# Low parts of streamed weights by adding transfers onto -hi, and attention scores of head pairs on two row halves of the array

## Chip, cores and metric

The kernel runs on one core of a Trainium2 chip. The metric is the device time of one execution in microseconds, the median of several runs. The engines are TensorE (PE; its weight loads are shown apart as PEld), VectorE (DVE), ScalarE (ACT), GpSimd (POOL) and SyncE (SP), which issues most transfers. PSUM is the memory that TensorE writes; SBUF holds everything else on the core.

## What is computed

Two layers of a hybrid block, for two request groups that share the weights: a prompt of 512 tokens and a sample group of 32 tokens with a past of 256. All of it is float32. Cut to what the change touches:

```python
h = rms_norm(x, g_mix)
glu_a, glu_b, rq, rk, rv, rg, fq, fk, fv, ff, gates = split_in(h @ w_in)
# A: GLU, causal depthwise conv (31 taps), LayerNorm, swish, w_conv_out
# B: retention, 8 heads, chunkwise, GroupNorm, gate, w_ret_out
# C: forgetting attention, 8 heads of 64:
fq = rms_norm(fq.reshape(b, t, H_FOX, DH_FOX), g_q_fox)
fk = rms_norm(fk.reshape(b, t, H_FOX, DH_FOX), g_k_fox)
s = jnp.einsum('bthd,bshd->bhts', q, k) * (DH_FOX ** -0.5)
s = jnp.where(mask, s + cum_q - cum_k, -jnp.inf)
p = jax.nn.softmax(s, axis=-1)
o = jnp.einsum('bhts,bshd->bthd', p, v)
# merged = sum of gated branches; x = x + merged @ w_out
# FFN: a, gb = split(rms_norm(x) @ w_ffn_up); x = x + (gelu(dwconv3(a)) * gb) @ w_ffn_down
```

## The kernel before

Activations lie transposed, channels on the 128 partitions and the T = 544 tokens (32 of the sample group, then 512 of the prompt) along the free dimension, so each matrix product is a row of gemms that give 128 output channels for all tokens.

**The gemms.** A float32 operand is used as two float32r values, hi (the value as ScalarE writes it to float32r) and lo = value - hi. `gemm` (L287) makes three passes for each of 8 blocks of 128x128 weights and each half of the tokens (272 columns): weight hi x activation hi, weight hi x activation lo, weight lo x activation hi. That is 48 matmuls (L305) into one PSUM tile `acc`, of which there are two.

**The weight stream.** `Stream` (L182) brings the weights in 146 units per layer, 1024 columns (512 KB) each, in the order of use. `load_part` (L190) loads a unit from the DRAM tensor `wpack` into `raw` (two buffers), issued by SyncE. `split_part` (L197) then fills `hi` and `lo` (three buffers each): ScalarE copies raw to hi (L203), and GpSimd subtracts hi from raw (L204). For the first two units VectorE subtracts. A `slot` (L311) takes unit u, asks for the split of unit u + 2 and the load of unit u + 4 (`ahead`, L225), and runs the gemm; so a unit's hi and lo are written while the gemm before the last runs, as soon as the gemm that used their buffers is over.

**The attention branch (C).** `qk_done` (L586) takes one of 4 + 4 gemm results (two heads of q or k each, on 64 partitions apiece), normalizes them, and splits the prompt part into hi and lo. For a matmul with 128 rows it stacks operands: SyncE copies hi and lo by four transfers per result into `qst[e]` (own half: q hi, other half: q lo) and `kst[e]` (k hi in both halves); the low part of k goes to `klo`. `p_scores` (L743) handles one head and one block of 128 queries: one matmul of 128 rows gives q hi x k hi + q lo x k hi (L751), a second one of 64 rows adds q hi x k lo (L752). The columns are the keys up to the block's end, at least 256. Then VectorE adds the bias and the mask (L755, L756), `softmax` runs on VectorE and ScalarE (L685), `p_trans` transposes (L763, copied out by ScalarE at L765) and `p_pv` multiplies by v (L781).

**What sets the order.** `fox_side` (L663) is a generator; its steps, and the conv of branch A (`conv_side`, L473, whose taps are L483 on VectorE), are called from hooks inside the gemms, two or three per gemm. In step k it runs the scores of item k, the transposes of item k - 3 and the product with v of item k - 4. The tile framework then places the instructions of each engine. ScalarE, VectorE and GpSimd each work through their own list in that order; SyncE does the same with its transfers. The retention side (L868 its scores, on row halves of the array; L892, L898, L904 its products) follows after the attention side.

Of the kernel before, what the change touches and what calls it, by code (L numbers as in the profile page):

```python
# [11 lines left out]
F32 = mybir.dt.float32  # L12
F32R = mybir.dt.float32r
AF = mybir.ActivationFunctionType
ALU = mybir.AluOpType
AX = mybir.AxisListType

P = 128
DEPTH = 2
D = 1024  # L20
NS = 32
NP = 512
T = NS + NP
# [88 lines left out]
def trunk(ctx, tc, x_in, wpack, wff, consts, params, s_conv, s_ret, s_cache, s_clf, s_ffn,  # L112
          y_out, o_conv, o_ret, o_fk, o_fv, o_lf, o_ffn):
    nc = tc.nc
    PS = bass.MemoryType.PSUM
    mm = nc.tensor.matmul
    act = nc.scalar.activation
    vtt = nc.vector.tensor_tensor
    stt = nc.vector.scalar_tensor_tensor
    gtt = nc.gpsimd.tensor_tensor  # L120
    dma = nc.sync.dma_start
# [12 lines left out]
    def Q(dt=F32):  # L134
        return qpool.tile([P, 4, T], dt, tag="q", name="q")

    def Wt(n=T):
        t = wpool.tile([P, CU], F32, tag="w", name="w")
        return t[:, :n]

    def Wr(n=T):
        t = wpool.tile([P, CU], F32R, tag="w", name="wr")
        return t[:, :n]
# [7 lines left out]
    def psS_t():  # L151
        return psS.tile([P, 512], F32, tag="s", name="s")
# [29 lines left out]
    class Stream:  # L182
# [14 lines left out]
        def split_part(self, u, i, sub, n=2):  # L197
            if i == 0:
                self.hl[u] = [upool.tile([P, UW], F32R, tag=t, name=t, bufs=3) for t in ("hi", "lo")]
                self.ns += 1  # L200
            hi, lo = self.hl[u]
            sl = slice(i * UW // n, (i + 1) * UW // n)
            act(hi[:, sl], self.raw[u][:, sl], AF.Copy)  # L203
            sub(lo[:, sl], self.raw[u][:, sl], hi[:, sl].bitcast(F32), op=ALU.subtract)  # L204
            if i == n - 1:
                self.raw.pop(u)

# [4 lines left out]
        def split(self, upto):  # L212
            while self.ns <= min(upto, DEPTH * NU - 1):
                self.load(self.ns)
                self.split_part(self.ns, 0, gtt, 1)

        def take(self):
            u = self.at
# [51 lines left out]
    def after(fn, lag=1):  # L270
        later.append([lag, fn])
# [39 lines left out]
    def slot(rhs, done, lo_last=False):  # L311
        blocks = ws.take()
        ws.ahead()
        tick()
        done(gemm(blocks, rhs, lo_last))
# [10 lines left out]
    def head_mean(src):  # L326

        hi, lo = Wr(), Wr()
        act(hi, src, AF.Copy)  # L329
        vtt(lo, src, hi.bitcast(F32), op=ALU.subtract)  # L330

        def product():
            res = []
            for h in range(2):
                p = psS_t()[:, :HN]
                mm(p, blkr, half(hi, h), start=True, stop=False)
                mm(p, blkr, half(lo, h), start=False, stop=True)
                res.append(p)
            return res

        return product

    def rsqrt(out, parts, m=1):

        y2 = Wt(out.shape[-1])
        n = parts[0].shape[-1]
        for i, v in enumerate(parts):
            act(out[:, i * n : (i + 1) * n], v, AF.Abs_reciprocal_sqrt, scale=1.0 / m, bias=epst)
        act(y2, out, AF.Square, scale=math.sqrt(0.5 / m))  # L349
        for i, v in enumerate(parts):  # L350
            y = y2[:, i * n : (i + 1) * n]
            stt(y, v, EPS * m, y, op0=ALU.add, op1=ALU.mult)  # L352
        stt(out, y2, 1.5, out, op0=ALU.subtract, op1=ALU.mult, reverse0=True)  # L353
# [71 lines left out]
    for l in range(DEPTH):  # L425
# [159 lines left out]

        def qk_done(j, gcol, out):  # L586
            def done(acc):
                qr = Wr()
                q = qr.bitcast(F32)
                R_norm.evict(q, acc)  # L590
                sq = Wt()
                act(sq, q, AF.Square)
                mean = head_mean(sq)

                def fin():
                    y = Wt()
                    rsqrt(y, mean())
                    stt(q, q, gcol, y, op0=ALU.mult, op1=ALU.mult)
                    is_k = out is not None
                    nc.gpsimd.tensor_copy(qks[:, is_k, j, :], q[:, 0:NS])  # L600
                    if is_k:
                        dma(out[:, j, :], q)
                        hi = Wr(NP)
                        act(hi, q[:, NS:T], AF.Copy)
                        gtt(klo[:, j, NS:T], q[:, NS:T], hi.bitcast(F32), op=ALU.subtract)
                    else:
                        hi, lo = Wr(NP), qr[:, NS:T]
                        act(hi, q[:, NS:T], AF.Copy)
                        gtt(lo, q[:, NS:T], hi.bitcast(F32), op=ALU.subtract)
                    for e in range(2):  # L610
                        own = slice(e * 64, e * 64 + 64)
                        far = slice(64 - e * 64, 128 - e * 64)
                        dst = (kst if is_k else qst)[e]
                        dma(dst[own, j, NS:T].bitcast(F32), hi[own].bitcast(F32))
                        dma(dst[far, j, NS:T].bitcast(F32), (hi if is_k else lo)[own].bitcast(F32))

                after(lambda: after(fin, 1), 1)

            return done
# [24 lines left out]
        gq8 = spool.tile([P, 1], F32, tag="gq8", name="gq8")  # L644
        nc.vector.tensor_scalar(gq8, pcol(P_GQ), 0.125, None, op0=ALU.mult)
        qks = Wt(8 * NS).rearrange("p (a j n) -> p a j n", a=2, j=4)
        qst = [Q(F32R) for _ in range(2)]
        for j in range(4):
            slot(rhs, qk_done(j, gq8, None))
        kst = [Q(F32R) for _ in range(2)]  # L650
        klo = Q(F32R)
        for j in range(4):
            slot(rhs, qk_done(j, pcol(P_GK), o_fk[l]))
        fv = vtile()
# [3 lines left out]
            slot(rhs, v_done(fv, fvs, j, o_fv[l]))  # L658


        foh, fol = qst

        def fox_side():  # L663
            cqs = spool.tile([P, 2], F32, tag="cqs", name="cqs", bufs=1)
            cks = [Wt(PAST + NS) for _ in range(2)]
            for g in range(2):
                for i in range(4):
                    h = g * 4 + i
# [73 lines left out]

            def p_scores(it):  # L743
                h, qb = it["h"], it["qb"]
                r = (h % 2) * 64
                n = (qb + 1) * P
                c = ck(h)
                p = psS_t()
                qs = qst[h % 2][:, h // 2, NS + qb * P : NS + n]
                nn = max(n, 256)  # L750
                mm(p[:, :nn], qs, kst[h % 2][:, h // 2, NS : NS + nn], start=True, stop=False)  # L751
                mm(p[:, :nn], qs[r : r + 64], klo[r : r + 64, h // 2, NS : NS + nn], start=False, stop=True)  # L752
                L = Wt(512)
                it["L"] = L
                stt(L[:, :n], c[:, :n], CM[:, h, qb : qb + 1], p[:, :n], op0=ALU.subtract, op1=ALU.subtract)  # L755
                vtt(L[:, n - P : n], L[:, n - P : n], cmask, op=ALU.add)  # L756
                softmax(L, n)
# [29 lines left out]
            for pr in range(4):  # L787
                for qb in range(4):
                    a = dict(f=(p_scores, p_trans, p_pv), h=2 * pr, qb=qb)
                    b = dict(f=(p_scores, p_trans, p_pv), h=2 * pr + 1, qb=qb)  # L790
                    a["mate"] = b
                    items += [a, b]
            n = len(items)
            for k in range(n + 4):
                for lag, f in ((4, 2), (3, 1), (0, 0)):
                    if 0 <= k - lag < n:
                        it = items[k - lag]
                        it["f"][f](it)
                yield
# [264 lines left out]
            side.append(ret_side())  # L1064
            side.append(gn_side())

        branch(2, qst)

        def need():
            drain(side)  # L1070
# [226 lines left out]
```

## Time and profile before

| | us |
|---|---|
| runs before (3) | 2033.06, 2039.91, 2041.58; median 2039.91 |
| profiled execution | 2039.84 |
| its span, first to last instruction | 2038.1 |
| busy: PE / DVE / POOL / ACT | 1969.1 / 1225.7 / 900.7 / 788.2 |
| mean granted TensorE clock | 0.991 |

The profile is one execution recorded by hardware. Busy is the time in which an engine has an instruction in work; matmuls overlap, and what they cost is read from start to start. The stretches of one layer are roughly, in the first: the input and the projections up to 125 us, the attention and retention sides beside their gemms from 125 to 420, the gates and the output projection to 575, and the FFN to 1025, where the second layer's first gemms follow. In a group's line stand the count, the busy time, the mean duration of one in ns, and the idle time of the engine ahead of them with what ended it; in a timeline the start, the duration, and in brackets the idle time ahead.

### The profile page before, as it was taken

The page shows a single profiled execution, that of the slowest core. Times are in us where ns is not written, and L with a number is a line of the kernel's source. Part 1 is how long each engine was busy: PE and PEld are TensorE (multiplying, and loading weights), DVE is VectorE, ACT ScalarE, POOL GpSimd, SP SyncE. Part 2 cuts the span into 40 slices and gives each one's busy share as a digit, 9 for nine tenths or more (in the row PEclk, how much of TensorE's full clock was granted, in tenths as well). Part 3 has the DMA queues.
Part 4 walks back from the last instruction along what each step waited for, and adds up shares of the span by engine and source line. Part 5 has one row for each costly group of instructions (what it writes and reads, how often), then busy time and mean ns, then how long its engine had stood idle before and what let it go on. Part 6 is the DMA issues. An engine that isn't in the chain of part 4 may idle for free.

```text
span 2038.1 us, 37239 instructions
## 1 busy us (share of the span) xinstructions
PE 1969.1 (97%) x15768; PEld 1913.6 (94%) x15768; DVE 1225.7 (60%) x1641; ACT 788.2 (39%) x1172; POOL 900.7 (44%) x580
## 2 busy tenths in 40 slices
PE   8999998999999999999999888989999999999999
PEld 7987888999999999999999877889999999999999
DVE  5587989666355660466326979995653656505640
ACT  4354552264334331233335445523452343313331
POOL 4463544244444444444444645432444344444442
PEclk9999999999999999999999999999999999999999
DMA  5353312122232222222433622112223322222232
GB/s 200 92 174 108 94 48 76 58 73 87 90 127 90 87 89 89 86 91 87 131 112 105 182 85 88 53 56 67 81 83 101 120 83 85 93 83 94 83 105 76
DMA packets 69075, 194.22 MB, mean 95 GB/s; under 512 B 14012, under 2 KB 15660, under 8 KB 68524
## 3 DMA queue, kind: packets, MB, share of 16 engines
q1 hardware_dynamic: 68908, 191.84, 29.2%
q8 instruction: 124, 2.03, 0.4%
q14 instruction: 43, 0.35, 0.1%
HBM read 169.07 MB, written 9.89 MB: 88 GB/s over the span
## 4 chain that ended last, share of the span: by engine, by line
PE 71%; DVE 22%; ACT 3%; issue 3%; DMA 1%; POOL 0%; SPq 0%; DVEq 0%; ACTq 0%; POOLq 0%
PE acc L305 68%; DVE w L483 10%; DVE w L756 1%; DVE q L324 1%; ACT hi L203 1%; DVE w L755 1%; DVE w L394 1%; DVE mn L687 1%; DVE w L353 1%; PE s L752 0%; DVE w L352 0%; DVE q L843 0%; ACT q L323 0%; DVE w L873 0%; DVE q L1019 0%
## 5 line engine op out<-in xcount | busy, mean ns | idle before, releaser
L305 PE MATMUL acc<-q,hi 128*128 128x272 f32 x9344 | 1789.6, 291 | 23.3 <-ACT q L323 9.0
L305 PEld LDWEIGHTS acc<-q,hi 128*128 128x128 f32 x9344 | 1475.3, 189 | 42.8 <-issue 9.4
L305 PE MATMUL acc<-q,lo 128*128 128x272 f32 x4672 | 1349.6, 289 | 0.0
L204 POOL TENSOR_TENSOR lo<-raw,hi 128x1024 fp32r<-128x1024 f32 x290 | 714.4, 2464 | 849.4 <-ACT hi L203 811.6
L305 PEld LDWEIGHTS acc<-q,lo 128*128 128x128 f32 x4672 | 883.0, 189 | 0.0
L203 ACT ACTIVATE hi<-raw 128x1024 fp32r<-128x1024 f32 (+1 forms) x293 | 309.4, 1056 | 735.4 <-PE acc L305 601.7
L483 DVE SCALAR_TENSOR_TENSOR w<-w,par 128x574 f32<-128x574 f32 x208 | 247.4, 1190 | 3.5
L1179 DVE TENSOR_TENSOR q<-acc,q 128x544 f32<-128x544 f32 x32 | 23.2, 725 | 208.9 <-PE acc L305 208.9
L1146 DVE SCALAR_TENSOR_TENSOR w<-w,par 128x546 f32<-128x546 f32 x44 | 93.6, 2128 | 42.9 <-ACT w L1145 42.9
L394 DVE TENSOR_TENSOR w<-acc,R 128x544 f32<-128x544 f32 x78 | 56.1, 720 | 95.5 <-PE acc L305 95.4
L321 DVE TENSOR_TENSOR q<-w,q 128x544 fp32r<-128x544 f32 x44 | 92.4, 2099 | 31.9 <-ACT q L320 31.9
L1148 ACT ACTIVATE w<-w 128x546 f32<-128x546 f32 x44 | 29.1, 662 | 129.7 <-DVE w L1147 129.6
L689 ACT ACTIVATE w<-w,mn 128x128 f32<-128x128 f32 (+4 forms) x68 | 38.0, 559 | 81.4 <-DVE mn L687 79.1
L324 DVE SCALAR_TENSOR_TENSOR q<-q,par 128x544 fp32r<-128x544 f32 x24 | 49.0, 2042 | 22.4 <-ACT q L323 22.4
L1141 POOL COPY fb<-w 128x2 f32<-128x2 f32 x44 | 8.1, 185 | 117.8 <-DVE w L1138 117.8
L1138 DVE TENSOR_TENSOR w<-acc,R 128x32 f32<-128x32 f32 x44 | 8.4, 192 | 83.2 <-PE acc L305 83.0
L813 POOL TENSOR_TENSOR w<-w,cst 128x544 f32<-128x544 f32 x16 | 26.2, 1641 | 65.7 <-DMA w<-q 59.7
L692 ACT ACTIVATE w<-w,rs 128x128 f32<-128x128 f32 (+4 forms) x68 | 37.9, 557 | 32.1 <-DVE rs L691 31.7
L490 POOL TENSOR_TENSOR w<-w 128x574 f32<-128x574 f32 x24 | 43.4, 1809 | 12.8 <-ACT w L486 11.2
L330 DVE TENSOR_TENSOR wr<-w,wr 128x544 fp32r<-128x544 f32 x24 | 27.2, 1133 | 33.3 <-ACT wr L329 33.3
L352 DVE SCALAR_TENSOR_TENSOR w<-s,w 128x272 f32<-128x272 f32 (+1 forms) x60 | 23.7, 436 | 38.1 <-ACT w L349 38.1
L1018 DVE SCALAR_TENSOR_TENSOR w<-w,acc 128x544 f32<-128x544 f32 x32 | 23.0, 720 | 37.3 <-PE acc L305 37.0
(207 smaller groups left out, 1563.2 us busy)
## 6 DMA issues: line engine op xcount, KB each, us to landing
raw<-in_wpack_dram SPq DMA_DIRECT2D x291, 512.0 KB, 3.3
q<-wr SPq DMA_DIRECT2D x64, 128.0 KB, 2.4
w<-in_x_dram SPq DMA_DIRECT2D x16, 272.0 KB, 4.2
w<-q SPq DMA_DIRECT2D x64, 68.0 KB, 3.0
ck<-cscr SPq DMA_DIRECT2D x16, 256.0 KB, 3.4
out_dram<-wr SPq DMA_DIRECT2D x8, 272.0 KB, 2.4
out_dram<-w SPq DMA_DIRECT2D x8, 272.0 KB, 2.6
xn<-q SPq DMA_DIRECT2D x8, 272.0 KB, 4.0
```

The costliest lines, as they stand in the source:

```text
L203: act(hi[:, sl], self.raw[u][:, sl], AF.Copy)
L204: sub(lo[:, sl], self.raw[u][:, sl], hi[:, sl].bitcast(F32), op=ALU.subtract)
L305: mm(acc[:, h, :HN], w, half(x, h), start=(i == 0 and j == 0), stop=(i == n - 1 and j == len(passes) - 1))
L321: vtt(lo, src, hi.bitcast(F32), op=ALU.subtract)
L324: stt(lo, src, scale, hi.bitcast(F32), op0=ALU.mult, op1=ALU.subtract)
L394: vtt(two(out), acc, two(self.R), op=ALU.mult)
L483: stt(c, u[:, k : k + CO], pcol(w + k), c, op0=ALU.mult, op1=ALU.add)
L490: gtt(p, p, t, op=ALU.add)
L689: act(L[:, :n], L[:, :n], AF.Exp, scale=-1.0, bias=mn, accum_out=sm)
L692: act(L[:, :n], L[:, :n], AF.Copy, scale=rs)
L1146: stt(c, a[:, 1 : 1 + FO], pcol(w + 1), c, op0=ALU.mult, op1=ALU.add)
L1148: act(c, c, AF.Gelu)
```

## The change

First, for all units but the first two, ScalarE writes hi and then lo = -hi (a second pass over 1024 columns, scale -1), and GpSimd issues a transfer that adds the unit's weights from DRAM onto lo. GpSimd's subtraction is gone; `raw` is read by ScalarE alone. Second, the stacked operands and the transfers that fill them are gone: q and k keep hi and lo in `qhl` and `khl`, and the even head's call of `p_scores` makes the scores of both heads of a pair by six matmuls of 64 rows, in turn on the upper and the lower half of the array, into two PSUM tiles. The product with v runs five steps behind instead of four, so the side has one step more.

```diff
@@ split_part, split
             act(hi[:, sl], self.raw[u][:, sl], AF.Copy)
-            sub(lo[:, sl], self.raw[u][:, sl], hi[:, sl].bitcast(F32), op=ALU.subtract)
+            if sub is None:
+
+                act(lo[:, sl], hi[:, sl].bitcast(F32), AF.Copy, scale=-1.0)
+                nc.gpsimd.dma_start(lo[:, sl], wpack[u][:, sl], accum_op=ALU.add)
+            else:
+                sub(lo[:, sl], self.raw[u][:, sl], hi[:, sl].bitcast(F32), op=ALU.subtract)
...
-                self.split_part(self.ns, 0, gtt, 1)
+                self.split_part(self.ns, 0, None, 1)
@@ qk_done
-                qr = Wr()
-                q = qr.bitcast(F32)
+                q = Wt()
...
-                        hi = Wr(NP)
-                        act(hi, q[:, NS:T], AF.Copy)
-                        gtt(klo[:, j, NS:T], q[:, NS:T], hi.bitcast(F32), op=ALU.subtract)
-                    else:
-                        hi, lo = Wr(NP), qr[:, NS:T]
-                        act(hi, q[:, NS:T], AF.Copy)
-                        gtt(lo, q[:, NS:T], hi.bitcast(F32), op=ALU.subtract)
-                    for e in range(2):
-                        own = slice(e * 64, e * 64 + 64)
-                        far = slice(64 - e * 64, 128 - e * 64)
-                        dst = (kst if is_k else qst)[e]
-                        dma(dst[own, j, NS:T].bitcast(F32), hi[own].bitcast(F32))
-                        dma(dst[far, j, NS:T].bitcast(F32), (hi if is_k else lo)[own].bitcast(F32))
+                    hi, lo = (khl if is_k else qhl)
+                    act(hi[:, j, NS:T], q[:, NS:T], AF.Copy)
+                    gtt(lo[:, j, NS:T], q[:, NS:T], hi[:, j, NS:T].bitcast(F32), op=ALU.subtract)
...
-        qst = [Q(F32R) for _ in range(2)]
+        qhl = [Q(F32R) for _ in range(2)]
...
-        kst = [Q(F32R) for _ in range(2)]
-        klo = Q(F32R)
+        khl = [Q(F32R) for _ in range(2)]
@@ p_scores
-                p = psS_t()
-                qs = qst[h % 2][:, h // 2, NS + qb * P : NS + n]
-                nn = max(n, 256)
-                mm(p[:, :nn], qs, kst[h % 2][:, h // 2, NS : NS + nn], start=True, stop=False)
-                mm(p[:, :nn], qs[r : r + 64], klo[r : r + 64, h // 2, NS : NS + nn], start=False, stop=True)
+                if h % 2 == 0:
+
+                    nn = max(n, 256)
+                    ps = [psS_t(), psS_t()]
+                    for i, (a, b) in enumerate(((0, 0), (0, 1), (1, 0))):
+                        for e in range(2):
+                            own = slice(e * 64, e * 64 + 64)
+                            mm(ps[e][:, :nn], qhl[a][own, h // 2, NS + qb * P : NS + n],
+                               khl[b][own, h // 2, NS : NS + nn], start=(i == 0), stop=(i == 2))
+                    it["p"], it["mate"]["p"] = ps
+                p = it["p"]
@@ fox_side, the steps
-            for k in range(n + 4):
-                for lag, f in ((4, 2), (3, 1), (0, 0)):
+            for k in range(n + 5):
+                for lag, f in ((3, 1), (5, 2), (0, 0)):
```

The order on three engines shows where it moves instructions. Line numbers of after differ by a few from those of before (L203 is the same; L206 and L207 are the two new lines; L310 is the gemm's matmul, L747 the scores', L761 the transposes', L779 the product with v, L1143 and L1146 the two ScalarE steps of the FFN that were L1145 and L1148, L325 the hi copy that was L320, L1139 and L1140 the small GpSimd copies that were L1141 and L1142).

ScalarE in the FFN of the first layer, before (hi, raw and lo are the weight stream's tiles, w and q working tiles):

```order
L203 ACTIVATE hi<-raw 128x1024
L1145 ACTIVATE w<-w,par 128x546
L1148 ACTIVATE w<-w 128x546
L203 ACTIVATE hi<-raw 128x1024
L320 ACTIVATE q<-w 128x544
```

and after:

```order
L203 ACTIVATE hi<-raw 128x1024
L206 ACTIVATE lo<-hi 128x1024
L1143 ACTIVATE w<-w,par 128x546
L1146 ACTIVATE w<-w 128x546
L203 ACTIVATE hi<-raw 128x1024
L325 ACTIVATE q<-w 128x544
L206 ACTIVATE lo<-hi 128x1024
```

Of each two units one has its lo right behind its hi, ahead of the FFN's steps; the other has it behind L325.

GpSimd at the same place, before:

```order
L204 TENSOR_TENSOR lo<-raw,hi 128x1024
L1141 COPY fb<-w 128x2
L204 TENSOR_TENSOR lo<-raw,hi 128x1024
L1142 COPY fb<-w 128x2
L1136 COPY w<-sf 128x2
L1137 MEMSET w 128x2
```

and after:

```order
L207 DMA lo<-in_wpack_dram 128x1024
L1139 COPY fb<-w 128x2
L1140 COPY fb<-w 128x2
L207 DMA lo<-in_wpack_dram 128x1024
L1134 COPY w<-sf 128x2
L1135 MEMSET w 128x2
```

Each transfer stands about where a subtraction stood; one of the small copies moved from behind the second to ahead of it.

TensorE in the attention side, before, at a block of 384 keys and the next (s is a PSUM tile of scores, t of transposes, o of the product with v; the gemm's matmuls between are left out by taking rows that follow each other):

```order
L781 MATMUL o<-w,q 64x128 x2
L763 MATMUL t<-cst,w 128x128 x2
L751 MATMUL s<-q 128x384
L752 MATMUL s<-q 128x384
L305 MATMUL acc<-q,hi 128x272 x2
L305 MATMUL acc<-q,lo 128x272
```

and after, at the next block, of 512 keys:

```order
L761 MATMUL t<-cst,w 128x128 x2
L779 MATMUL o<-w,q 64x128 x2
L747 MATMUL s<-q 128x512 x6
L310 MATMUL acc<-q,hi 128x272 x2
L310 MATMUL acc<-q,lo 128x272
```

The two matmuls per head became six per pair of heads, with nothing between them here; the next head's turn brings none, and the transposes moved ahead of the product with v. Of the 32 groups of six in the program, six are cut: into three and three with other rows between (four of them), or into three, two and one (two).

More of the change, by code (lines that the diff above doesn't have):

```diff
@@ L658, in trunk @@
             slot(rhs, v_done(fv, fvs, j, o_fv[l]))
-        foh, fol = qst
+        foh, fol = qhl
         def fox_side():
@@ L744, in p_scores @@
                 h, qb = it["h"], it["qb"]
-                r = (h % 2) * 64
                 n = (qb + 1) * P
                 c = ck(h)
-                p = psS_t()
-                qs = qst[h % 2][:, h // 2, NS + qb * P : NS + n]
-                nn = max(n, 256)
-                mm(p[:, :nn], qs, kst[h % 2][:, h // 2, NS : NS + nn], start=True, stop=False)
-                mm(p[:, :nn], qs[r : r + 64], klo[r : r + 64, h // 2, NS : NS + nn], start=False, stop=True)
+                if h % 2 == 0:
[8 more added lines that the diff above has]
+                p = it["p"]
                 L = Wt(512)
@@ L1065, in start_ret @@
             side.append(gn_side())
-        branch(2, qst)
+        branch(2, qhl)
         def need():
```

## Prediction

> **What bounds the kernel now.** I read the page's first part and its chain, then the busy table by stretch, then what TensorE waits for.
>
> ```profile
> span 2038.1 us, 37239 instructions
> ...
> PE 1969.1 (97%) x15768; PEld 1913.6 (94%) x15768; DVE 1225.7 (60%) x1641; ACT 788.2 (39%) x1172; POOL 900.7 (44%) x580
> ...
> PE acc L305 68%; DVE w L483 10%; DVE w L756 1%; DVE q L324 1%; ACT hi L203 1%; DVE w L755 1%; DVE w L394 1%; DVE mn L687 1%; DVE w L353 1%; PE s L752 0%; DVE w L352 0%; DVE q L843 0%; ACT q L323 0%; DVE w L873 0%; DVE q L1019 0%
> ```
>
> TensorE is the bound: it is idle for 2038.1 - 1969.1 = 69 us of the span. The change leaves the matmuls of the big gemms (L305) as they are. In the chain the only other entry of weight is VectorE's conv step L483.
>
> ```profile
> core 0: us, PE busy (x) PEld busy (x) DVE busy (x) ACT busy (x) POOL busy (x), PEclk, DMA share, GB/s
> 125.00:420.00 295.00, 273.32 (x2256) 249.54 (x2255) 247.29 (x354) 128.62 (x251) 128.42 (x65) 0.97 0.27 84
> 630.00:1025.00 395.00, 395.00 (x3151) 394.84 (x3151) 189.60 (x232) 129.39 (x153) 178.38 (x153) 1.00 0.29 96
> 1135.00:1430.00 295.00, 270.18 (x2250) 245.45 (x2249) 248.53 (x353) 127.01 (x248) 127.67 (x64) 0.98 0.27 83
> ```
>
> In the FFN (630 to 1025) TensorE has no gap: 395 us / 3151 = 125.4 ns a matmul, 6.01 us for a gemm of 48. Nothing can be won there; much can be lost. What can be won lies in the two attention stretches (one per layer), where TensorE is idle 21.7 + 24.8 = 46.5 us and VectorE is busy 84%.
>
> ```profile
> PE s L701 <- DVE w L712: 10.2, 2, 5.2
> PE acc L305 <- ACT q L323: 9.0, 3, 6.1
> PE t L763 <- ACT w L765: 8.7, 7, 2.3
> PE acc L305 <- DVE w L394: 8.5, 6, 2.5
> PE s L631 <- DVE w L352: 7.3, 2, 3.7
> ```
>
> TensorE's own waits (total, times, longest). The three ended by VectorE come to 26.0 us; those on ScalarE's L765 are copies between two transposes.
>
> **Part 1, the low parts.** Now ScalarE makes hi and GpSimd subtracts; then ScalarE makes hi and -hi, and GpSimd only issues a transfer that adds the weights from DRAM onto -hi.
>
> ```profile
> 710.58 1.06 ACT L203 ACTIVATE hi<-raw 128x1024 fp32r<-128x1024 f32 x1 [0.38 <-PE acc L305]
> 711.89 0.66 ACT L320 ACTIVATE q<-w 128x544 fp32r<-128x544 f32 x1 [0.25 <-DVE w L1160]
> ```
>
> ```profile
> 705.70 2.40 POOL L204 TENSOR_TENSOR lo<-raw,hi 128x1024 fp32r<-128x1024 f32 x1 [0.62 <-ACT hi L203]
> ```
>
> ```profile
> 706.47 2.21 DVE L1146 SCALAR_TENSOR_TENSOR w<-w,par 128x546 f32<-128x546 f32 x1 [0.97 <-ACT w L1145]
> 708.72 0.79 DVE L1147 SCALAR_TENSOR_TENSOR w<-w,par 128x546 f32<-128x546 f32 x1
> ```
>
> ```profile
> raw<-in_wpack_dram SPq DMA_DIRECT2D x291, 512.0 KB, 3.3
> ```
>
> *Cover.* A hi starts when a gemm ends and frees one of the three buffers; its unit is used two gemms later, 12.0 us in the FFN. In the order of after, every second lo follows its hi directly (2 x 1.06 us, leaving 9.9 us for the transfer) and every second one stands behind L325 (L320 before): that ends at 712.55, lo at 713.6, 3.0 us after its hi began, leaving 9.0 us. A transfer of these 512 KB that only writes lands in 3.3 us. One that also reads its destination is in no row. Its ends: 3.3 us (it can't beat the plain one) and three plain ones in a row, 9.9 us (read, read, write). I take two, 6.6 us, the nearest row once for the source and once for the destination: it hides under the 9.0 us and costs nothing. Without that cover each microsecond beyond it costs half a microsecond per gemm.
>
> The Trainium skill ("DMA: Bandwidth & Descriptors", section "Anatomy of one DMA") fits a GpSimd-issued transfer by 2.0 us plus bytes / 436e9, which makes 3.2 us of this size; by an estimate from that page with the bytes counted twice, 4.4 us. The sum would be the same.
>
> *The 16 DMA engines* are busy 0.29 of the FFN with one plain transfer per gemm. At twice a plain one the added transfer makes 0.29 x 3 = 0.87: it fits. From 2.4 plain ones on ((1 - 0.29) / 0.29) they are the bound.
>
> ```profile
> 125.00:420.00 295.00, 0.00 (x0) 77.61 (x32) 0.97 0.27 84
> ```
>
> ```profile
> 21.54 2.40 POOL L204 TENSOR_TENSOR lo<-raw,hi 128x1024 fp32r<-128x1024 f32 x1 [4.52 <-ACT hi L203]
> ```
>
> ```profile
> 25.70 0.41 PE L305 MATMUL acc<-q,hi 128*128 128x272 f32 x2
> ...
> 28.47 1.18 PE L386 MATMUL s<-ss,ones 128*128 128x272 f32 x4 [1.11 <-DVE ss L376]
> ```
>
> The first row is the subtractions alone (L204, GpSimd's busy time and count) in the first attention stretch. *ScalarE* gets 290 passes (2 x 146 units less two) of 1.06 = 307 us: 788 + 307 = 1095 us, 54% of the span; 32 of them fall in a stretch (128.6 + 34 = 163 of 295 us). A lo ahead of L765 delays a transpose by up to 1.06 us; for the 7 waits on L765 I add **4 us**, about half of that (ends 0 and 10). At the start the first unit treated in the new way has little cover: its subtraction ends at 23.94 and its gemm starts at 25.70. ScalarE's second pass and a transfer of 6.6 us, in place of 2.4, end about 5.3 us later; 1.8 us are cover and 1.1 us are waited for at L386 anyway: **+2 us** (ends 0 and 5).
>
> *GpSimd* loses 714 us of subtractions. It keeps its order: each transfer stands where the subtraction stood, one ScalarE pass later, and small copies wait behind it as they did.
>
> *VectorE* gains. L1146 ran beside GpSimd's subtraction and took 2.21 us; L1147, of the same shape, ran behind it and took 0.79. In the attention stretches:
>
> ```profile
> L483 DVE SCALAR_TENSOR_TENSOR w<-w,par x208: 793/818/3011, 127.4 to 1387.5; 128x574 f32<-128x574 f32 x104
> ```
>
> ```profile
> L483 DVE SCALAR_TENSOR_TENSOR w<-w,par 128x574 f32<-128x574 f32 x208 | 247.4, 1190 | 3.5
> ```
>
> Mean less median is 372 ns x 208 = 77 us for L483. GpSimd's other work stays; 77.6 of its 128.4 us in a stretch are subtractions, so about 0.6 of the 77 goes: 46 us of VectorE time. What TensorE gets of it lies between 0 and all 46.5 us of idle. I take half, **-23 us**: the three waits on VectorE are 26.0 us, and each is a queue of L483 ahead of what TensorE wants; what is late next is ScalarE.
>
> Against this speaks a rule of the Trainium skill ("SBUF — State Buffer", the box on the "DVE blocks DMA" trap): while VectorE runs an instruction that takes both of its ports, GpSimd can't write the descriptors of a transfer that it issues. No run here shows it. It is a reason for the first rival.
>
> **Part 2, the scores.** Two matmuls per head and block (128 rows, then 64) become six per pair of heads, each on 64 rows, in turn on the upper and lower half.
>
> ```profile
> 199.16 0.48 PE L751 MATMUL s<-q 128*128 128x512 f32 x1
> 199.57 0.50 PE L752 MATMUL s<-q 64*128 64x512 f32 x1
> 200.00 0.51 PE L305 MATMUL acc<-q,hi 128*128 128x272 f32 x2
> ...
> 206.88 0.36 PE L751 MATMUL s<-q 128*128 128x256 f32 x1
> 207.17 0.38 PE L752 MATMUL s<-q 64*128 64x256 f32 x1
> 207.48 0.52 PE L305 MATMUL acc<-q,hi 128*128 128x272 f32 x2
> ...
> 356.48 1.16 PE L868 MATMUL s<-q 64*128 64x128 f32 x16
> 357.57 0.52 PE L305 MATMUL acc<-q,hi 128*128 128x272 f32 x2
> ...
> 629.75 1.18 PE L386 MATMUL s<-ss,ones 128*128 128x272 f32 x4 [0.27 <-DVE ss L376]
> 630.57 0.61 PE L305 MATMUL acc<-q,hi 128*128 128x272 f32 x2
> ```
>
> From start to start the two take 0.60 us at 256 columns and 0.84 at 512: 0.12 us per 256 columns and matmul, and 0.18 us each for going between 128 and 64 rows. A head has blocks of 256, 256, 384 and 512 columns: 0.60 + 0.60 + 0.72 + 0.84 = 2.76 us, x 16 = 44 us now. After, a group of six changes twice (0.36). If the halves run side by side, three times the streaming is left: 0.72, 0.72, 0.90, 1.08 = 3.42 us per pair, x 8 = 27 us. One after the other: 5.40 x 8 = 43 us. L868 already uses the halves in turn: 16 records of 128 columns in 1.09 us, 0.18 of it the change, so 57 ns each; L386, on all rows, takes from 629.75 to the next matmul at 630.57, 205 ns for 272 columns, 96 ns for 128. So they overlap, and I take 27. In the order of after three of 16 groups per layer are cut in two by other work and lose the overlap and one more change: 6 x 0.72 = 4 us. **-13 us** (ends 0 and -17). The 64 copies into stacked operands go from SP's queue; nothing on TensorE waited for them in the rows above.
>
> **Sum.** Profiled execution 2039.8 us (span 2038.1), the median of the runs is 2039.9: 2039.8 - 13 - 23 + 2 + 4 = 2009.8, so **2010 us**.
>
> **Rivals.** (1) *The adding transfers come late* (slower). Place: every gemm of 6.0 to 6.5 us, about 234 (the 1448 us outside the stretches). It decides from 9 us of landing, or 2.4 plain transfers of engine time. At 9.9 us every second gemm waits (9.9 - 9.0) / 2 = 0.45 us, 53 us in all: 2063; at three plain ones of engine time 0.29 x 4 = 1.16, 6.97 us a gemm, 0.96 x 234 = +225 us: 2235. Against it: 6.6 us by the nearest rows. For it: no row shows such a transfer. Chance 0.25. (2) *The halves don't overlap and VectorE's gain stays off TensorE's path*: 2039.8 - 1 + 4 + 6 = about 2045, at best 2030; for it, the waits named are a tenth of VectorE's busy time; against it, L868. 0.13. (3) *VectorE sets the pace of the stretches*, as the 10% of L483 in the chain say: most of the 46 us goes, 1980. 0.12.
>
> **Chances.** Forecast 0.50 (1992 to 2030). What a measurement can tell from no change is about 0.5%, 10 us. Faster 0.50 + 0.12 = 0.62, the same 0.13, slower 0.25. The range runs from 1975 to 2060: rivals 2 and 3 are in it and the near end of rival 1.
>
> **What would show it.** Right: the FFN at 125.4 ns a matmul with no wait of TensorE for lo's transfer; L483's mean near 0.9 us; L1146 near 0.8; six score matmuls of 256 columns in 0.7 us. Wrong: transfers landing after 9 us or a DMA share near 1 in the FFN (rival 1); six in 1.08 us (rival 2); TensorE idle in the stretches still near 46 us.

## The result and the profile after

The changed kernel takes **1994.67 us** (median of 4 runs, 1988.49 to 1999.15) where the kernel before takes 2039.67 (4 runs, 2033.06 to 2041.58): a ratio of 0.9779, 95% interval 0.9761 to 0.9797, so 45 us less. The forecast was 2010, its range 1975 to 2060. The profiled execution of after is the slowest of its four (1999.15 us), so the two traces differ by 41 us of span only.

The page of after, first part and chain:

```profile
span 1997.0 us, 37750 instructions
...
PE 1951.2 (98%) x15832; PEld 1909.6 (96%) x15832; DVE 950.5 (48%) x1641; ACT 1062.5 (53%) x1462; POOL 425.3 (21%) x580
...
PE acc L310 75%; DVE w L488 3%; DMA lo<-in_wpack_dram 1%; PE s L747 1%; DMA w<-q 1%; PE o L779 1%; DVE w L754 1%; PE t L761 1%; DVE w L753 1%; POOL lo L207 1%; DMA w<-cscr 0%; DVE mn L680 0%; POOL w L377 0%; ACT lo L206 0%; PE s L866 0%
```

The conv step (L488, L483 before) fell from 10% of the chain to 3%. VectorE does the same 1641 instructions in 950.5 us instead of 1225.7. Two of its groups, the conv step and a step of the FFN, in count, busy time and mean ns:

```profile
L488 DVE SCALAR_TENSOR_TENSOR w<-w,par 128x574 f32<-128x574 f32 x208 | 198.4, 954 | 3.8
...
L1144 DVE SCALAR_TENSOR_TENSOR w<-w,par 128x546 f32<-128x546 f32 x44 | 34.7, 788 | 83.5 <-ACT w L1143 83.5
```

The second one before, over all its 44 instructions (the conv step took 1190 ns):

```profile
L1146 DVE SCALAR_TENSOR_TENSOR w<-w,par 128x546 f32<-128x546 f32 x44 | 93.6, 2128 | 42.9 <-ACT w L1145 42.9
```

The FFN of the first layer, in the columns of the stretches above, and what the transfers do (median us from issue to landing; a queue's share of the 16 engines over the span):

```profile
630.00:1025.00 395.00, 395.00 (x3153) 394.84 (x3152) 124.36 (x227) 193.44 (x220) 74.41 (x148) 1.00 0.82 184
```

```profile
q0 software_dynamic: 41760, 152.06, 45.6%
q1 hardware_dynamic: 63788, 183.44, 27.8%
```

```profile
raw<-in_wpack_dram SPq DMA_DIRECT2D x291, 512.0 KB, 3.4
lo<-in_wpack_dram POOLq DMA_DIRECT2D x290, 512.0 KB, 5.5
```

The FFN is still without a gap (395 / 3153 = 125.3 ns a matmul). The adding transfers land in 5.5 us against 3.4 for plain ones of the same bytes, and the engines are busy 0.82 of the FFN. TensorE's largest waits are now:

```profile
PE acc L310 <- ACT q L328: 7.6, 3, 6.2
PE s L747 <- DVE w L753: 5.8, 4, 3.0
PE acc L310 <- DMA lo<-in_wpack_dram: 5.4, 1, 5.4
PE t L761 <- ACT w L763: 5.1, 4, 1.9
```

The wait of L701 on L712 (10.2 us before) is gone from the top; a single wait of 5.4 us for a low part is new.

Where the time went is seen stage by stage, if the stages are cut by work and not by the clock: below, a layer is cut where its 8th, 20th, 36th, 52nd, 72nd and 80th gemm end (counted by their matmuls, to within a gemm), and the time between those points is read from each trace, first layer / second layer. Three experiments stand beside. Each column is one execution.

| gemms of a layer | before | scores only | transfers only | after | after without transfers |
|---|---|---|---|---|---|
| 0-8, first part of the input | 58.2 / 49.8 | 58.2 / 49.8 | 66.1 / 49.3 | 66.7 / 49.3 | 57.9 / 49.3 |
| 8-20, q, k, v | 86.7 / 86.2 | 84.6 / 84.6 | 83.8 / 83.4 | 84.3 / 84.3 | 79.2 / 79.9 |
| 20-36, attention side | 165.5 / 166.4 | 168.5 / 164.0 | 157.9 / 152.1 | 153.0 / 150.6 | 151.2 / 152.2 |
| 36-52, retention side | 131.6 / 132.0 | 130.9 / 131.3 | 123.8 / 123.8 | 123.8 / 123.7 | 123.8 / 123.8 |
| 52-72, branches | 125.7 / 127.3 | 127.2 / 127.3 | 126.0 / 127.5 | 127.5 / 127.6 | 123.6 / 123.6 |
| 72-80, w_out | 49.2 / 49.2 | 49.2 / 49.2 | 48.4 / 48.4 | 48.4 / 48.4 | 48.4 / 48.4 |
| 80-146, FFN | 400.1 / 399.9 | 400.2 / 399.9 | 399.5 / 399.4 | 399.5 / 399.4 | 399.5 / 399.4 |

After gains 44 us in the attention and retention stages, 4 in the q, k, v stage, loses 8.4 at the start, and changes little elsewhere.

### The profile page after: what moved, and what is told of

It reads as the page before. It is cut to its first block, busy times and chain, and to the rows that moved or that the text cites. A ratio compares the mean times of both kernels' runs of the same rounds, so it can differ in the third digit from the quotient of the medians.

```text
span 1997.0 us, 37750 instructions
## 1 busy us (share of the span) xinstructions
PE 1951.2 (98%) x15832; PEld 1909.6 (96%) x15832; DVE 950.5 (48%) x1641; ACT 1062.5 (53%) x1462; POOL 425.3 (21%) x580
## 3 DMA queue, kind: packets, MB, share of 16 engines
q0 software_dynamic: 41760, 152.06, 45.6%
q1 hardware_dynamic: 63788, 183.44, 27.8%
## 4 chain that ended last, share of the span: by engine, by line
PE 80%; issue 6%; DVE 6%; ACT 2%; DMA 2%; POOL 2%; SPq 1%; DVEq 0%; POOLq 0%; ACTq 0%
PE acc L310 75%; DVE w L488 3%; DMA lo<-in_wpack_dram 1%; PE s L747 1%; DMA w<-q 1%; PE o L779 1%; DVE w L754 1%; PE t L761 1%; DVE w L753 1%; POOL lo L207 1%; DMA w<-cscr 0%; DVE mn L680 0%; POOL w L377 0%; ACT lo L206 0%; PE s L866 0%
## 5 line engine op out<-in xcount | busy, mean ns | idle before, releaser
L310 PE MATMUL acc<-q,hi 128*128 128x272 f32 x9344 | 1791.3, 291 | 12.7 <-ACT q L328 7.6
L310 PEld LDWEIGHTS acc<-q,hi 128*128 128x128 f32 x9344 | 1478.4, 190 | 27.1 <-ACT q L328 8.7
L310 PE MATMUL acc<-q,lo 128*128 128x272 f32 x4672 | 1352.2, 290 | 5.7 <-DMA lo<-in_wpack_dram 5.4
L310 PEld LDWEIGHTS acc<-q,lo 128*128 128x128 f32 x4672 | 884.4, 190 | 6.8 <-DMA lo<-in_wpack_dram 6.3
L203 ACT ACTIVATE hi<-raw 128x1024 fp32r<-128x1024 f32 (+1 forms) x293 | 309.8, 1057 | 655.5 <-PE acc L310 654.0
L207 POOL DMA_DIRECT2D lo<-in_wpack_dram x290 | 251.7, 868 | 1264.6 <-ACT lo L206 1174.9
L206 ACT ACTIVATE lo<-hi 128x1024 fp32r<-128x1024 f32 x290 | 305.1, 1052 | 4.4
L488 DVE SCALAR_TENSOR_TENSOR w<-w,par 128x574 f32<-128x574 f32 x208 | 198.4, 954 | 3.8
L399 DVE TENSOR_TENSOR w<-acc,R 128x544 f32<-128x544 f32 x94 | 67.7, 720 | 120.2 <-PE acc L310 118.4
L1144 DVE SCALAR_TENSOR_TENSOR w<-w,par 128x546 f32<-128x546 f32 x44 | 34.7, 788 | 83.5 <-ACT w L1143 83.5
L1146 ACT ACTIVATE w<-w 128x546 f32<-128x546 f32 x44 | 29.1, 662 | 70.5 <-DVE w L1145 70.5
L326 DVE TENSOR_TENSOR q<-w,q 128x544 fp32r<-128x544 f32 x44 | 31.9, 725 | 33.7 <-ACT q L325 33.7
L753 DVE SCALAR_TENSOR_TENSOR w<-ck,CM,s 128x128 f32<-128x128 f32 (+3 forms) x64 | 34.3, 536 | 13.4 <-PE s L747 13.4
```

The source lines that it names most:

```text
L206: act(lo[:, sl], hi[:, sl].bitcast(F32), AF.Copy, scale=-1.0)
L207: nc.gpsimd.dma_start(lo[:, sl], wpack[u][:, sl], accum_op=ALU.add)
L310: mm(acc[:, h, :HN], w, half(x, h), start=(i == 0 and j == 0), stop=(i == n - 1 and j == len(passes) - 1))
L399: vtt(two(out), acc, two(self.R), op=ALU.mult)
L488: stt(c, u[:, k : k + CO], pcol(w + k), c, op0=ALU.mult, op1=ALU.add)
L1144: stt(c, a[:, 1 : 1 + FO], pcol(w + 1), c, op0=ALU.mult, op1=ALU.add)
```

## Experiments

Times are medians; each ratio is against the kernel before, run beside it.

### The two parts apart

The first kernel has the new `split_part` and the old scores; the second the new scores and the old subtraction:

```diff
# transfers only: before, with
-                self.split_part(self.ns, 0, gtt, 1)
+                self.split_part(self.ns, 0, None, 1)
# scores only: after, with
-                self.split_part(self.ns, 0, None, 1)
+                self.split_part(self.ns, 0, gtt, 1)
```

> The adding transfers alone, with the scores of before. Theory A (GpSimd's reads of SBUF slowed VectorE in the attention stretches, and this is the larger part of the gain): 28 to 32 us under before, about 2010 us; the conv step's mean (1190 ns before, 954 ns after) near 950 ns; TensorE idle in the two stretches about 25 us less than before. Theory B (most of the gain comes from the scores, whose groups free TensorE and the working tiles around them): 10 to 15 us under before, about 2027 us, with the conv step as short all the same. The two parts add up to the 45 us of the whole within 5 us if neither hides the other.

> The scores by row halves alone, with GpSimd's subtractions. Theory A: 11 to 17 us under before, about 2026 us (the score groups 44 us to about 30, nothing else), the conv step's mean near 1190 ns, GpSimd's subtraction ahead of it as before. Theory B: 30 us or more under before, about 2010 us.

Transfers only: 2006.21 us, ratio 0.9839 (0.9822 to 0.9856), 32 us less. Scores only: 2037.09, ratio 0.9992 (0.9982 to 1.0003), no difference. Together they give 45, so they are not additive: the scores are worth nothing alone and 11.5 us (2006.2 to 1994.7) once the transfers are in. That step is one between medians; the two profiled executions differ by 2.8 us only (spans of 1999.8 and 1997.0), since the one of transfers only is the fastest of its runs and the one of after the slowest. The attention stage of the first layer (gemms 20 to 36) shows why. In the order before, scores only, transfers only, after, one row each (the stretch, its length, busy times of PE, PEld, DVE, ACT, POOL, granted clock, DMA share, GB/s):

```profile
151.00:316.00 165.00, 154.99 (x1180) 135.93 (x1179) 141.96 (x225) 81.56 (x181) 75.76 (x39) 0.96 0.27 83
```

```profile
149.00:317.00 168.00, 148.90 (x1212) 133.83 (x1211) 142.98 (x229) 81.44 (x181) 76.37 (x39) 0.95 0.25 79
```

```profile
156.00:314.00 158.00, 152.84 (x1186) 132.78 (x1185) 123.53 (x230) 95.51 (x197) 48.10 (x39) 1.00 0.61 145
```

```profile
157.00:310.00 153.00, 146.15 (x1216) 132.40 (x1216) 121.29 (x232) 95.68 (x198) 49.56 (x39) 0.98 0.60 142
```

The score groups take about 6 us of TensorE's busy time away in both pairs (155.0 to 148.9, and 152.8 to 146.2). Beside the subtractions VectorE stays at 142 us, 86% of the stage, and the 6 us become idle time: 10.0 us of TensorE's before, 19.1 with the scores only. Beside the transfers VectorE needs 20 us less, and the stage shrinks by 5 us (by 1.5 in the second layer). So VectorE, and not TensorE, sets the pace there as long as GpSimd subtracts. Theory A is right on the larger part, and wrong on the scores alone (11 to 17 us were expected).

### What of GpSimd slows VectorE

To after, GpSimd's old operation is added again, its result unused; or, in its place, two operations that only write:

```diff
                 nc.gpsimd.dma_start(lo[:, sl], wpack[u][:, sl], accum_op=ALU.add)
# subtraction (first version; second: the same inside tc.keep_in_program_order)
+                gtt(self.raw[u][:, sl], self.raw[u][:, sl], hi[:, sl].bitcast(F32), op=ALU.subtract)
# two writes
+                for _ in range(2):
+                    nc.gpsimd.memset(self.raw[u][:, sl], 0.0)
```

> The kernel after, in which GpSimd also subtracts hi from raw, in place, behind each transfer that it issues; the result is read by nobody. The transfers stay. Theory A: the conv step's mean goes back to about 1190 ns, the FFN's second VectorE step to about 2.1 us, and the time rises by 20 to 30 us, to about 2020. Rival C (the gain came because GpSimd's list is short, so that its small copies and the low parts come sooner, not from VectorE): a rise too, but the VectorE steps stay near 954 and 788 ns. Rival D (the gain came from the transfers being ready earlier than the subtractions): no rise, within 4 us of 1995.

> The kernel after, in which GpSimd sets raw to zero twice behind each transfer, an operation that writes and reads nothing; some 2 us per unit. Theory A, if it is GpSimd's reading: the conv step's mean stays near 954 ns and the time within 4 us of 1995. If any use of SBUF by GpSimd does it: conv step and time as with the subtraction. Rival C (the length of GpSimd's list): the same rise as with the subtraction, with VectorE's steps short.

> As the kernel after with GpSimd's extra subtraction in raw, but with the order on GpSimd held: first the transfer of a unit, then its subtraction (in the run before it the scheduler had put the subtraction first, so that each transfer left 2.4 us or more later). Theory A (VectorE is slowed by GpSimd's reading, and VectorE sets the pace of the attention stretches): VectorE's conv step near 1150 ns again and the time at the level of the scores alone (2037 us) plus what the start costs (8 us), about 2035 to 2045. Rival E (most of the 130 us lost in the run before it came from VectorE as well, by more than the subtraction cost before the change): 2100 or more again. Rival D (VectorE's pace doesn't matter, late transfers did it all): 1995 to 2005 though the conv step is at 1150 ns.

Two writes: 2010.72 us, ratio 0.9867 (0.9851 to 0.9883). Subtraction: 2126.18, 1.0426 (1.0408 to 1.0443). Subtraction behind its transfer: 2168.53, 1.0643 (1.0619 to 1.0667). The conv step in the three, in that order:

```profile
L490 DVE SCALAR_TENSOR_TENSOR w<-w,par 128x574 f32<-128x574 f32 x208 | 196.2, 943 | 3.8
```

```profile
L489 DVE SCALAR_TENSOR_TENSOR w<-w,par 128x574 f32<-128x574 f32 x208 | 240.8, 1158 | 3.8
```

```profile
L489 DVE SCALAR_TENSOR_TENSOR w<-w,par 128x574 f32<-128x574 f32 x208 | 270.4, 1300 | 3.8
...
L1145 DVE SCALAR_TENSOR_TENSOR w<-w,par 128x546 f32<-128x546 f32 x44 | 183.2, 4164 | 105.3 <-ACT w L1144 105.3
```

GpSimd is busy longer with the two writes (961.7 us in all) than it was before (900.7), and VectorE is as fast as in after; with GpSimd's subtraction back, VectorE's step is as slow as before. So it isn't how long GpSimd is busy; what the subtraction does beyond the writes is to read two tiles. The timeline of the last kernel shows how (start, duration):

```profile
725.10 2.71 POOL L208 TENSOR_TENSOR raw<-raw,hi 128x1024 f32<-128x1024 f32 x1
...
727.00 4.91 DVE L1145 SCALAR_TENSOR_TENSOR w<-w,par 128x546 f32<-128x546 f32 x1 [2.04 <-ACT w L1144]
...
727.69 1.20 POOL L207 DMA_DIRECT2D lo<-in_wpack_dram  x1
728.30 3.01 POOL L208 TENSOR_TENSOR raw<-raw,hi 128x1024 f32<-128x1024 f32 x1
```

A VectorE step of 0.79 us begins at 727.00 and ends at 731.91, 0.6 us after the second subtraction ended (731.31): it is not slowed, it waits until GpSimd is through, two subtractions and a transfer's issue long. The Trainium skill says this of the two engines ("SBUF — State Buffer", section "Who interferes with whom"): a VectorE operation with two inputs in SBUF contends with a GpSimd operation that reads SBUF and not with one that only writes it, and whoever is first holds the shared port for the whole instruction. The traces agree, with 943 ns beside writes and 1158 to 1300 beside reads.

What the times say is less clean. Both versions with the subtraction lose far more than the 20 to 50 us that theory A gave them. In the first the transfers land in 7.0 us instead of 5.5 and leave behind the subtraction; in the second they land in 5.5 us as in after, and VectorE is busy 1368.3 us, 143 more than before. So rival E holds for the second (VectorE's own loss exceeds that of before) and rival D falls with it, while the first was confounded by late transfers. The two writes cost 16 us without slowing VectorE, and their transfers land in 7.0 us; what the 16 us come from was not taken apart. These 16 us are the most that can be put down to the length of GpSimd's list (rival C).

### The score groups

The first trace of the row halves, in after: a group of six with 256 columns, and one that other work cuts in two.

```profile
202.36 0.61 PE L747 MATMUL s<-q 64*128 64x256 f32 x3
202.91 0.52 PE L310 MATMUL acc<-q,hi 128*128 128x272 f32 x2
...
209.98 0.62 PE L747 MATMUL s<-q 64*128 64x256 f32 x6
210.53 0.52 PE L310 MATMUL acc<-q,hi 128*128 128x272 f32 x2
210.89 0.29 PE L310 MATMUL acc<-q,lo 128*128 128x272 f32 x1
```

Six take 0.55 us to the next matmul, and that pair takes 0.36 where it takes 0.25 elsewhere: 0.66 with both changes between 64 and 128 rows (0.72 forecast). Three alone take the same 0.55: a cut group pays twice. To see whether the turn between halves matters, three matmuls of the upper half were put ahead of three of the lower:

```diff
-                    for i, (a, b) in enumerate(((0, 0), (0, 1), (1, 0))):
-                        for e in range(2):
+                    for e in range(2):
+                        for i, (a, b) in enumerate(((0, 0), (0, 1), (1, 0))):
```

> The kernel after, with the six score matmuls of a pair in another order: three on the upper half, then three on the lower. Theory (halves overlap only where they alternate): a group of 256 columns takes from start to next gemm matmul about 0.9 to 1.0 us where it takes 0.55, of 512 columns 1.6 where it takes 0.90; 16 us of TensorE time in all, of which up to 16 us show in the time: 2000 to 2011. Rival (the order doesn't matter, or the saving is not there): groups as long as after, within 3 us of 1995.

1997.80 us, ratio 0.9798 (0.9778 to 0.9819), not to be told from after. The group of six in its trace:

```profile
205.38 0.62 PE L747 MATMUL s<-q 64*128 64x256 f32 x6
205.93 0.52 PE L310 MATMUL acc<-q,hi 128*128 128x272 f32 x2
```

0.55 us again. In the records the matmuls of such a group start in three pairs, the two of a pair 10 ns apart (4 ns in after), though the program has three of one half first (the tile framework keeps that order in 26 of the 32 groups). My theory that halves overlap only in turn falls; the cut groups point to other work between the two halves as what costs the overlap.

### What the transfers cost

One version without them, one with the first half of the columns added once more, and one that starts as before:

```diff
# without
-                nc.gpsimd.dma_start(lo[:, sl], wpack[u][:, sl], accum_op=ALU.add)
# half more
                 nc.gpsimd.dma_start(lo[:, sl], wpack[u][:, sl], accum_op=ALU.add)
+                nc.gpsimd.dma_start(lo[:, : UW // 2], wpack[u][:, : UW // 2], accum_op=ALU.add)
# start as before
-                self.split_part(self.ns, 0, None, 1)
+                self.split_part(self.ns, 0, gtt if self.ns < 5 else None, 1)
```

> The kernel after without the adding transfers: ScalarE still writes hi and -hi, nothing is added onto -hi, so the weights' low parts are left out of the result (from unit 2 on). GpSimd neither subtracts nor issues. Theory (the transfers cost nothing once the kernel runs; what they cost is the start): the FFN as long as after (399.5 us), the attention stretches within 3 us of after, the first eight gemms back at about 58 us, in all 8 us less: about 1987 us. Rival (the transfers' load on the 16 engines, or GpSimd's 868 ns for each issue, delays other transfers and small copies in the attention stretches): 10 us or more beyond that, 1975 or less.

> The kernel after with the adding transfer of the first 512 columns made once more, behind the first one, so the low parts hold these weights' value a second time. Theory (the cover of 9.0 to 9.9 us sets the limit): two transfers one after the other land about 5.5 + 1 + 4 = 10.5 us after the first issue; 1.0 us late on average, half of it per gemm, 0.5 us x 234 = 120 us: about 2115. If the 16 engines are the limit: 0.29 + 0.53 x 1.5 = 1.08 of the FFN's time, 6.5 us a gemm there: about 2105 as well, but with a share of the engines near 1.0 in the FFN. Rival (there is far more room than the forecast said): within 20 us of 1995, no wait for the low parts.

> The kernel after with GpSimd's subtraction for units 2, 3 and 4, and the adding transfer from unit 5 on. Theory: the first eight gemms take 66.7 us after and 58.2 before; 5.4 us of it is the one wait for the low part of unit 2, and some 3 us is the lower clock granted behind that wait (0.66 from 30 to 40 us). With the subtraction both go: 8 us less, about 1987 us, and the clock from 30 to 40 us near 1.00. Rival 1: only the wait goes, 5 us. Rival 2: the 1.6 MB of constants still fill the transfer engines from 30 to 42 us, and unit 5 or 6 waits in place of unit 2: no gain within 2 us.

**Without transfers**: 1971.73 us, ratio 0.9669 (0.9653 to 0.9684), so in after they cost 23 us, with all that goes with them: GpSimd's issues (251.7 us in all) are gone too, and VectorE's conv step is at 917 ns. The stage table has it: 8.8 at the start, 5.1 and 4.4 in the q, k, v stages, 3.9 and 4.0 in the branches, nothing in the FFN, next to nothing beside the attention. One way in which they cost outside the start is seen in a transfer that ScalarE waits for. The results' transfers land in 4.7 us in after and in 2.7 without (the same lines of the two pages):

```profile
out_dram<-w SPq DMA_DIRECT2D x16, 272.0 KB, 4.7
```

```profile
out_dram<-w SPq DMA_DIRECT2D x16, 272.0 KB, 2.7
```

and the timeline of after has ScalarE held up by one:

```profile
140.12 0.78 ACT L491 ACTIVATE w<-w,par 128x574 f32<-128x574 f32 x1 [3.55 <-DMA out_dram<-w]
```

That this is all of it was not tried.

**Start as before**: 1987.58 us, ratio 0.9754 (0.9734 to 0.9775). Its first eight gemms take 59.2 us instead of 66.7, and the clock granted from 30 to 40 us is 1.00 instead of 0.66, as the theory had it. The start of after, on TensorE:

```profile
27.34 0.41 PE L310 MATMUL acc<-q,hi 128*128 128x272 f32 x2
33.14 0.59 PE L310 MATMUL acc<-q,lo 128*128 128x272 f32 x1 [5.39 <-DMA lo<-in_wpack_dram]
33.53 0.65 PE L310 MATMUL acc<-q,hi 128*128 128x272 f32 x2
...
38.07 0.66 PE L310 MATMUL acc<-q,hi 128*128 128x272 f32 x2
...
39.15 0.42 PE L310 MATMUL acc<-q,hi 128*128 128x272 f32 x2
```

Unit 2's transfer was issued at 24.2 and TensorE waits for it until 33.1; the loads of the next units and, from 30.5 on, of 1.6 MB of constants go through the same engines. Behind the wait a pair takes 0.65 us instead of 0.41 until 38.5. The Trainium skill ("TensorE: Matmul & The Clock Gate", section "What's actually happening") has the array's clock halved after about 3.4 us of idling; the rows agree in kind, and the slow spell lasts 5.4 us (4.5 us behind the same wait in the version with the halves apart, 31.1 to 35.6). The ratios' intervals of this version and after overlap; the stage's 7.5 us don't rest on them.

**Half more**: 2529.20 us, ratio 1.2403 (1.2327 to 1.2479), more than four times the loss that either sum gave. Its waits, of GpSimd and TensorE:

```profile
POOL lo L208 <- DMA lo<-in_wpack_dram: 1726.6, 280, 9.0
PE acc L311 <- DMA lo<-in_wpack_dram: 390.4, 215, 13.0
```

The second transfer, onto the same tile, waits on GpSimd until the first has landed, 6.2 us on average, and everything behind it on GpSimd waits too, the next unit's first transfer included. So a unit's transfers take a whole gemm's period (565.4 / 66 = 8.6 us in the FFN) and can't run beside the next unit's; my price of half a microsecond per late microsecond assumed that they can. The engines' share is 0.75 there: not their limit.

### ScalarE's pass, the steps, the rotation

```diff
# before, with one pass more
+            act(lo[:, sl], hi[:, sl].bitcast(F32), AF.Copy, scale=-1.0)
             sub(lo[:, sl], self.raw[u][:, sl], hi[:, sl].bitcast(F32), op=ALU.subtract)
# start as before, with the old steps
-            for k in range(n + 5):
-                for lag, f in ((3, 1), (5, 2), (0, 0)):
+            for k in range(n + 4):
+                for lag, f in ((4, 2), (3, 1), (0, 0)):
# start as before, rotation on VectorE
-                        gtt(w, w, sinT, op=ALU.mult)
+                        vtt(w, w, sinT, op=ALU.mult)
-                        gtt(q, q, w, op=ALU.add)
+                        vtt(q, q, w, op=ALU.add)
```

> The kernel before, in which ScalarE also writes lo = -hi ahead of GpSimd's subtraction, which overwrites it: ScalarE's second pass alone, 290 passes of 1.06 us. The prediction's term for it was 4 us (0 to 10): 2039 plus 4. Rival: 2 x 1.06 us ahead of the evictions lengthens VectorE's and GpSimd's lists too, more than 10 us. Rival: ScalarE has room everywhere, 0 within 2 us.

> The version with the subtraction for units 2 to 4 (1987.6 us), with the old steps of the attention side: product with v four steps behind and ahead of the transposes. Theory (the order of these steps costs or gains little; the change's gain in the scores is the overlap alone): within 3 us of 1987.6. Rival (the fifth step is needed, since the scores of a pair now come in one step and the next two steps are crowded): 5 to 10 us slower, with longer waits of TensorE for ScalarE's copies between transposes.

> The version with the subtraction for units 2 to 4 (1987.6 us), in which VectorE also does the two products and sums of the rotation that GpSimd did (16 x 2 operations of 1.5 to 1.9 us, in the attention stretch). Theory (a VectorE operation on two SBUF operands waits for the end of a GpSimd operation of this kind, whatever the rest): the conv step's mean falls from 940 to about 850 ns (208 x 90 ns = 19 us), and VectorE takes on 32 x 0.72 = 23 us; about even, 1984 to 1991. Rival (VectorE no longer sets the pace anywhere, so that its added work is hidden and the shorter chain of the rotation counts): 5 us or more faster. Rival (VectorE still sets the pace and the waits don't shrink): 10 us slower.

**One pass more**: 2062.33 us, ratio 1.0114 (1.0096 to 1.0131), 23 us more, nearly six times my term. But it isn't ScalarE's time alone: GpSimd's subtraction stands behind the pass here and comes later, and VectorE's conv step beside it grows from 1190 to 1253 ns. What the pass costs in after is not told apart by this.

**Old steps**: 1991.20 us, ratio 0.9763 (0.9745 to 0.9781): 3.6 us above the version it is made from, where within 3 were expected and 5 to 10 by the rival. The intervals overlap, so no difference is to be told.

**Rotation on VectorE**: 1973.14 us, ratio 0.9682 (0.9663 to 0.9701), the best of all: 14 us under its parent and 67 under the kernel before.

```profile
PE 1937.0 (98%) x15832; PEld 1898.1 (96%) x15832; DVE 955.6 (48%) x1673; ACT 1060.1 (54%) x1459; POOL 377.4 (19%) x548
...
L488 DVE SCALAR_TENSOR_TENSOR w<-w,par 128x574 f32<-128x574 f32 x208 | 190.4, 915 | 3.7
```

VectorE takes on 32 operations (24.9 us by their rows) and is busy 5 us longer than its parent's 950.5: it won back 20 us elsewhere, only 5 of them in the conv step, where the theory had 19. The balance on VectorE came as expected, the even time did not: at 14 us it is the first rival that fits. The time fell in the attention stages (153.0 / 148.4 to 144.8 / 146.4). Whether the rotation's shorter chain or VectorE's fewer waits did it is open.

## Why the forecast was right, and where it was off

The sign and both mechanisms were right; the sizes of three terms were off, and the terms were not independent.

- **VectorE's relief, -23: too small.** Transfers only gain 38 us in the attention and retention stages (7.7 + 14.3 + 7.9 + 8.2). Taking half of TensorE's 46.5 us of idle was the weak choice: of the 37.0 us of idle in these four stages 27.7 went, three quarters, and TensorE's busy time fell by 10.3 besides. The retention stages gained 8 us each though VectorE was busy only 75% there before (98.36 of 132 us), and the granted clock rose with the waits gone (0.96 to 1.00 in the attention stage's rows), which the sum had not. The forecast's conv step of 0.9 us is 0.95, and its 0.8 for L1146 (L1144 after) is 0.79. Rival 3 (VectorE sets the pace of the stretches) described them better than the forecast did.
- **Scores, -13: right as TensorE's work, wrong as time.** The work shrank by 6.7 + 6.0 = 12.7 us (152.8 to 146.2 in the row above, 150.6 to 144.6 in the second layer). The time it brings depends on the other term: nothing beside the subtractions, 11.5 us beside the transfers. Adding the two terms as if they were independent was the fault: 32 and 1.5 us apart, 45 together. That this term came out near its size was luck in that sense: the other part stood in the same change.
- **The start, +2: 8.4** (58.2 to 66.7; the version with the halves apart, which starts in the same way, took 63.8). The step took a landing of 6.6 us; it was 8.9 us, and behind the wait of 5.4 us the lower clock cost some 3 us more.
- **The transfer, 6.6 us and free: 5.5 us and free in the FFN.** The share of 0.87 came out at 0.82. It was not free elsewhere: 17 us in the q, k, v and branch stages against a kernel without it, by slower small transfers among others, which the sum had not considered. Since the subtractions had a price there too, little of it shows against before.
- **ScalarE's pass, +4: not settled.** Waits on L763 fell from 8.7 to 5.1 us rather than grew.
- **Rival 1** needed landings above 9 us as a rule; they run from 5.0 to 9.1 us with a median of 5.5, and TensorE waited for one of them, at the start. **Rival 2** asked for halves that don't overlap; six matmuls took 0.55 us, not 1.08. Its other half, that VectorE's gain stays off TensorE's path, falls with the 32 us of the transfers alone. Its sum is also misadded: 2039.8 - 1 + 4 + 6 is 2049, not 2045. **Rival 3**'s 1980 is more than its own terms give: even all of the 46 us makes 2039.8 - 13 - 46 + 6 = 1987. Both stay inside the range.
- **The rule weighed against the change** (VectorE keeping GpSimd from issuing) doesn't show: the 290 issues took 0.86 to 1.01 us. The 123 that ran beside a step of VectorE with two inputs in SBUF took 870 ns on average, the others 866; no COPY and no TENSOR_SCALAR of VectorE ran beside an issue, so for those it stays open.

## What to carry to other kernels

Ask of a saving on the bound engine whether another engine sets the pace of that stretch; if so it can be worth nothing until that engine is relieved, as the scores were here. GpSimd's subtraction, which reads SBUF, held VectorE's two-input steps up until it was through, so work that a transfer, or VectorE itself, can do is worth moving even where GpSimd has time to spare. An adding transfer of 5.5 us fits under two gemms of 6 us once the stream runs; for the first units, and for anything that waits for a small transfer, count what it does to the rest of the traffic.

## What the runs showed of the hardware that was not expected

- An adding transfer of 512 KB lands in 5.5 us and the adding transfers keep the engines busy 1.6 times as long as the queue of the other transfers (45.6% against 27.8% of the span, for 152.06 against 183.44 MB counted), so about twice as long per megabyte.
- Matmuls on the two row halves start in pairs even where the program lists three of one half first (10 ns apart, and 0.55 us for six as in turn).
- A VectorE operation of 0.79 us lasted up to 4.91 us behind two GpSimd subtractions.
